# A layer of attention, convolution and feed-forward on one core: transfers in program order, and value products in three 64-column parts

## Chip, cores and metric

The kernel runs on one core of a Trainium2 chip. The metric is the device time of one execution in microseconds (us). A core has TensorE (PE in the profile), VectorE (DVE), ScalarE (ACT), GpSimd (POOL) and SyncE (SP), which here does nothing but issue DMA transfers. Weight loads of TensorE have a row of their own, PEld.

## What is computed

One layer over 2048 tokens of width 1024: an RMSNorm, one projection to three groups of heads, a norm per head on what they give, an output projection, a residual sum, then a second RMSNorm and a SwiGLU feed-forward part of width 2816. Four heads do stick-breaking attention over all earlier keys, eight heads do softmax attention over a band of 576 keys with a bias that depends on distance, and 256 channels pass a short gated convolution.

```
h = rmsnorm(x, attn_norm_w); q_a, k_a, v_a, q_b, k_b, v_b, g_b, g_c, x_c = split(h @ w_in)
y = concat(stick_breaking(q_a, k_a, v_a), chunked_relpos(norm(q_b), norm(k_b), v_b, rel_bias), short_conv(g_b, g_c, x_c))
x = x + group_rmsnorm(y) @ w_out
x = x + (silu(r @ w_gate) * (r @ w_up)) @ w_down,   r = rmsnorm(x, ffn_norm_w)
```

## The kernel before

Numbers of 32 bits are carried as pairs of 16-bit numbers, a high and a low part, and a product is made of three: high by high, high by low, low by high. The tokens lie in reverse order, in four groups of 512 or sixteen tiles of 128, and the attention part works in two halves of two groups each.

Two things are woven together (`weave`, L941). One is the stream of projections (`fill`, L900): for each half the values, queries and keys, the convolution, then the output projection of the first half (`out_proj`, L858). The other is a line of attention pieces (`attend`, L788): a stick-breaking tile of 128 queries is cut into pieces of up to four key blocks (`stick_tile`, L713), a softmax tile is one piece of up to five (`chunk_tile`, L754). Half 0 has 112 pieces and half 1 has 176, so there are 288. A stage (`stage`, L978) has three beats; with each beat every open piece that is due is carried on by one step, and then a third of the stage's share of projection work is written down. A planned clock counts the cost of that work, and `later` (L895) puts something off until the planned clock is so much further. In this part PE's instructions run in the order in which they are written down; the line that says so is

```
with tc.manual_schedule(engines={mybir.EngineType.PE}):
    weave()
```

The streams of all other engines, SP among them, are ordered by the framework's scheduler, which may take a later load ahead of an earlier store that is not ready. When the weaving is over, `stream.paced` is false and the feed-forward part (`ffn`, L1020) and the output projection of the second half are written down plainly and ordered by the scheduler.

A softmax piece runs so: scores in PSUM (L704, L707), bias and maximum on VectorE (L766), exponential on ScalarE (L773), the reciprocal of the row sum times a scale into `f` (L777, L778), then `turned` (L650): PE transposes the weights into one of two `tp` banks (L660), ScalarE copies the high part (L664), VectorE makes the low part (L669) and with it frees the bank. `weighted` (L673) multiplies by the values: for each block of 128 keys the high weights by both parts of the values side by side, 128 columns (L679), and the low weights by the values' high part, 64 columns (L684). The `av` bank, of which there is one, then has two halves. `put_y` (L689) copies it to `yu` with the factor `f` on ScalarE (L694), which frees the bank, adds the halves on GpSimd (L696) and issues the store to `ydr` (L697). `yu` has two buffers, `f` has four.

Transfers that the steps below speak of: at a head's start `attend` issues K (L798, L800), V (L801, L803), the bias of a softmax head (L806), and for each group four transfers of q (L818); scores that use them are written down two beats later. `Rows` (L420) fetches blocks of x (L478), of the normed y (L486) or of the residual (L881), and they are squared (L368), scaled (L373) and transposed (L329). `Weights` (L204) loads a block of a weight two blocks ahead (L223), squares it (L249), splits it (L274 to L276), stores the parts (L277) and reads them back in the second half (L236). Stores: q, k parts (L533), v parts (L553), the convolution (L643), normed y (L844) and the residual (L872), for which x is loaded at L868. Squares of q and k are made on GpSimd (L579) and summed on VectorE (L583).

Of the kernel before, what the change touches and what calls it, by code (L numbers as in the profile page):

```python
# [20 lines left out]
HD = 64  # L21
# [19 lines left out]
def trunk(ctx: ExitStack, tc: tile.TileContext, x, anw, w_in, qnw, knw, biasx, conv_w, onw, w_out,  # L41
# [162 lines left out]
    class Weights:  # L204
# [22 lines left out]
        def split(self, n):  # L227

            if n >= len(self.plan) or n in self.ready:
                return  # L230
            key = self.plan[n]
            if key in wd and n not in self.raw:
                made = []
                for t in wd[key]:
                    w = wp.tile([128, 2, D], F16, name="w16", tag="w16")
                    nc.sync.dma_start(w, t)  # L236
                    made.append(w)
                self.ready[n] = made
                return
            self.load(n)  # L240
            shape, one, gain, srcs = block(key)
            tiles = self.raw.pop(n)
            self.ready[n] = made = []
            m = len(tiles)
            c = 1 if one else m
            ss = small(2, "ws", BF16)
            for i, raw in enumerate(tiles):
                with nc.allow_low_precision(reason="a bound, to a factor of two"):
                    nc.scalar.activation(junk(), raw, AF.Square, accum_out=ss[:, i:i + 1])  # L249
            yield 3.0  # L250
            o, bk = tpb()
            if one:
                for i in range(m):
                    nc.tensor.matmul(o[:, 0:1], ones, ss[:, i:i + 1], start=i == 0, stop=i == m - 1)
            else:
                nc.tensor.matmul(o[:, 0:m], ones, ss[:, 0:m], start=True, stop=True)
            t = small(2, "wt")
            sc = small(2, "wsc")
            nc.vector.tensor_scalar(t[:, :c].bitcast(I32), o[:, :c].bitcast(I32), 24, None,
                                    op0=ALU.logical_shift_right)  # L260
            nc.vector.tensor_scalar(sc[:, :c].bitcast(I32), t[:, :c].bitcast(I32), -1.0, 204.0,
                                    op0=ALU.mult, op1=ALU.add)
            nc.vector.tensor_scalar(sc[:, :c].bitcast(I32), sc[:, :c].bitcast(I32), 23, None,  # L263
                                    op0=ALU.logical_shift_left)
            ds = consts.tile([128, 2], F32, name=f"ds{len(DS)}")
            nc.vector.reciprocal(ds[:, :c], sc[:, :c])
            nc.vector.tensor_scalar(ds[:, :c], ds[:, :c], INV[gain], None, op0=ALU.mult)
            bk.done = True
            DS[key] = ds, one
            wd[key] = [dp.tile([128, 2, D], F16, name=f"wd{len(wd)}_{i}") for i in range(m)]  # L270
            for i, raw in enumerate(tiles):
                yield 1.5
                w = wp.tile([128, 2, D], F16, name="w16", tag="w16")
                nc.scalar.activation(raw, raw, AF.Copy, scale=sc[:, 0:1] if one else sc[:, i:i + 1])  # L274
                nc.scalar.copy(w[:, 0, :], raw)  # L275
                nc.gpsimd.tensor_tensor(w[:, 1, :], raw, w[:, 0, :], ALU.subtract)  # L276
                nc.sync.dma_start(wd[key][i], w)  # L277
                made.append(w)

        def start(self, n, after=0.0):  # L280
# [202 lines left out]
    def y_rows(H, groups):  # L483
# [4 lines left out]

        return Rows(H, groups, fetch)

    def behind(what):
        if stream.paced:
            later(0.8, what)
        else:
            what()
# [10 lines left out]
                           lambda k: hl[:, k, :], KT)  # L506
            behind(bk.read(lambda g=g, o=o: use(g, o)))

    def proj_N(H, groups, units, use, prep=None):

        for g in groups:
            hh, hl = H.get(g, (None, None))
            for t in range(0, 4, 2):
                if prep is not None:
                    yield from prep.need(g, t)
                    hh, hl = H[g]
                o, bk = acc()
                steps = chain.from_iterable(
                    mm3(o[:, s * 256:(s + 1) * 256], lambda k, cs=cs: hh[:, k, cs],
                        lambda k, cs=cs: hl[:, k, cs], lambda k: units[k // 4][0][:, k % 4],  # L520
# [5 lines left out]
    def put_parts(src, pair, g, d, scale):  # L526

        half, c = where(g)
        st = ap.tile([128, 2, 520], F16, name="st", tag="w2")[:, :, :GRP]
        nc.scalar.activation(st[:, 0, :], src, AF.Copy, scale=scale)  # L530
        nc.vector.scalar_tensor_tensor(st[:, 1, :], src, scale, st[:, 0, :], op0=ALU.mult, op1=ALU.subtract)
        for part in range(2):
            nc.sync.dma_start(d[pair, half, part][:, c:c + GRP], st[:, part, :])  # L533

    def v_block(H, groups, W, c0, head0, prep=None):

# [7 lines left out]
        def use(g, t, o):  # L544
# [5 lines left out]
                                           op0=ALU.mult, op1=ALU.subtract)  # L550
            hf, c = where(g)
            b = c // 128 + t
            nc.sync.dma_start(vd[head0, hf][:, b:b + 2], st)  # L553

        yield from proj_N(H, groups, units, use, prep)

# [49 lines left out]
    def conv_block(H, groups, W, b, between=None):  # L606
# [28 lines left out]
        def finish(g, t1):  # L635
# [4 lines left out]
            nc.scalar.copy(yc[:, :512], tp)  # L640
            bk.done = True
            for i in range(4):
                nc.sync.dma_start(ydr[g * 4 + i][:, 768 + 128 * b:896 + 128 * b], yc[:, i * 128:(i + 1) * 128])  # L643

        u = W.get(("cx", b))
        yield from proj_T(H, groups, u[0], use_gc)
# [25 lines left out]

    def weighted(av, wh, wl, vs, first, last):  # L673


        n = len(vs)

        def high(i):
            nc.tensor.matmul(av, wh[:, i * 128:(i + 1) * 128], vs[i], start=first and i == 0,  # L679
                             stop=last and i == n - 1 > 0)  # L680

        high(0)
        for i, v in enumerate(vs):
            nc.tensor.matmul(av[:, :HD], wl[:, i * 128:(i + 1) * 128], v[:, 0, :], start=False,  # L684
                             stop=last and n == 1)
        for i in range(1, n):
            high(i)

    def put_y(T, head, av, f):  # L689
        av, bk = av  # L690
        yield
        bk.done = True
        u = ap.tile([128, 2 * HD], F32, name="yu", tag="yu")
        nc.scalar.activation(u, av, AF.Copy, scale=f)  # L694
        yield
        nc.gpsimd.tensor_tensor(u[:, :HD], u[:, :HD], u[:, HD:], ALU.add)  # L696
        nc.sync.dma_start(ydr[T][:, head * HD:(head + 1) * HD], u[:, :HD])  # L697

    def scores(Q, cols, K, k0, n, diagonal=False):

# [7 lines left out]
        return z[:, :n], bk  # L708

    def open_av():  # L710
        return bank("av", 1, 2 * HD)

    def stick_tile(T, head, K, k0, Q, V, cols):  # L713

# [39 lines left out]
    def chunk_tile(T, head, K, k0, Q, V, cols, bias):  # L754
# [3 lines left out]
        def steps():  # L758
# [14 lines left out]
            nc.scalar.activation(s[:, :n * 128], s[:, :n * 128], AF.Exp, bias=nm, scale=qks[:, 1:2],  # L773
                                 accum_out=tot)
            yield 2
            f = small(1, "f")
            nc.vector.reciprocal(f, tot)  # L777
            nc.vector.tensor_tensor(f, f, VS[head], ALU.mult)  # L778
            yield 3
# [52 lines left out]
    def y_norm(T, yt, gain, tmp):  # L832
# [8 lines left out]
        yv = yt.rearrange("p (n d) -> p n d", d=HD)  # L841
        nc.vector.tensor_tensor(yv, yv, r[:, :, None].to_broadcast([128, 16, HD]), ALU.mult)
        nc.gpsimd.tensor_tensor(yt, yt, gain, ALU.mult)
        nc.sync.dma_start(ynd[T], yt)  # L844

    def y_norms(half):
        assert traced[half] == 0, (half, traced)
# [10 lines left out]
    def out_proj(H, groups, W, prep, rows):  # L858

        for g in groups:  # L860
            for cb in range(4):
                cc = slice(cb * 256, (cb + 1) * 256)
                units = W.get(("o", cb))

                def use(g, t, o, cb=cb, cc=cc):
                    xs = xp.tile([128, 2, 256], F32, name="xs", tag="xs", bufs=2)
                    T = g * 4 + t
                    nc.sync.dma_start(xs, x[T * 128:T * 128 + 256, cc].rearrange("(b p) c -> p b c", p=128))  # L868
                    nc.vector.scalar_tensor_tensor(xs, o.rearrange("p (b c) -> p b c", b=2),
                                                   descale(("o", cb), 0), xs, op0=ALU.mult, op1=ALU.add)  # L870
                    for b in range(2):
                        nc.sync.dma_start(x1d[T + b][:, cc], xs[:, b, :])  # L872

                yield from proj_N(H, [g], units, use, prep if cb == 0 else None)
                if g == groups[-1] and cb in (1, 2) and len(groups) > 1:
                    yield from rows.ahead()

# [128 lines left out]
    with tc.tile_pool(name="ap", bufs=1) as ap0:  # L1006

        class _Pool:
            BUFS = dict(k=2, q=4, be=5, re=2, w2=8, wth=3, wtl=3, v=2, vst=1, yu=2, bias=2)

            def tile(self, shape, dt, name, tag):
                return ap0.tile(shape, dt, name=name, tag=tag, bufs=self.BUFS[tag])

        ap = _Pool()
        with tc.manual_schedule(engines={mybir.EngineType.PE}):
            weave()

    fp = ctx.enter_context(tc.tile_pool(name="fp", bufs=1))
# [121 lines left out]
```

## Time and profile before

| what | us |
|---|---|
| median of three runs | 2697.05 (2690.57 to 2703.49) |
| the profiled execution, its own time | 2698.59 |
| its span, first to last instruction | 2696.8 |
| PE busy in the span | 2526.3 |
| VectorE, ScalarE, GpSimd busy | 1458.7, 1074.8, 398.8 |
| mean granted TensorE clock, share of full | 0.982 |

An engine's busy time in a stretch is read beside the stretch's length. The table of waits names an engine's instruction, what ended its wait, the total, the times and the longest wait. The timeline has one line for each instruction or for several of the same line in a row: start, time, engine, line, operation, what is written from what; a wait of the engine just before stands in brackets. A matmul's time is that of one product from its start to its end, and products overlap, so the distance between starts tells the pace.

### The profile page before, as it was taken

What the parts mean: (1) busy time and instruction counts of PE and PEld (TensorE: products, weight loads), DVE (VectorE), ACT (ScalarE), POOL (GpSimd) and SP (SyncE); (2) the same over time, 40 slices, a digit from 0 to 9 for tenths busy, and PEclk for the clock granted to TensorE, in tenths of its full rate; (3) what the DMA queues carried; (4) which work ended last, traced back from release to release, by engine and by line L of the source; (5) the groups of instructions that cost most, each with busy time, mean ns of one, the idle gap of its engine ahead of it and who ended that gap; (6) DMA issues with size and microseconds to landing.
All of it is one profiled execution on the core that took longest, in us unless ns stands there. A gap on an engine that the chain in (4) does not pass through costs nothing.

```text
span 2696.8 us, 41816 instructions
## 1 busy us (share of the span) xinstructions
PE 2526.3 (94%) x16258; PEld 1687.1 (63%) x16258; DVE 1458.7 (54%) x3343; ACT 1074.8 (40%) x1994; POOL 398.8 (15%) x469
## 2 busy tenths in 40 slices
PE   6998889998799888979999999999999999999999
PEld 4477766666686677745555555557865555555556
DVE  6478777689988977834444334334332333223233
ACT  5575756666456776752333333321121111111110
POOL 2234331102312122121111111110000000000000
PEclk9999999999999999989999999999999999999999
DMA  7443444533321356472222233222651111111101
GB/s 260 133 131 100 132 134 143 142 110 124 105 81 43 97 152 198 120 268 105 94 94 94 94 103 113 90 102 107 223 194 39 47 47 51 66 47 48 47 24 63
DMA packets 245350, 294.31 MB, mean 109 GB/s; under 512 B 77472, under 2 KB 194208, under 8 KB 245152
## 3 DMA queue, kind: packets, MB, share of 16 engines
q1 hardware_dynamic: 245152, 291.65, 33.5%
q8 instruction: 127, 2.08, 0.3%
q14 instruction: 71, 0.58, 0.1%
HBM read 199.30 MB, written 92.27 MB: 108 GB/s over the span
## 4 chain that ended last, share of the span: by engine, by line
PE 38%; DMA 4%; issue 4%; DVE 2%; POOL 1%; ACT 1%; SPq 1%; POOLq 0%; DVEq 0%; ACTq 0%
PE acc L381 7%; PE acc L380 7%; PE acc L379 7%; PE sc L1057 5%; PE sc L1058 5%; PE sc L1059 5%; DMA x1d<-xs 1%; POOL w L276 1%; DMA wr<-in_w_down 1%; DMA wr<-in_w_up 1%; DMA xf<-x1d 0%; PE sc L329 0%; DVE gl L1042 0%; DVE x L1061 0%; DVE wl L314 0%
## 5 line engine op out<-in xcount | busy, mean ns | idle before, releaser
L381 PE MATMUL acc<-hh,w 128*128 128x512 f16 x1728 | 656.3, 380 | 0.8 <-POOL w L276 0.8
L379 PE MATMUL acc<-hh,w 128*128 128x512 f16 x1728 | 656.5, 380 | 0.4 <-ACT hh L332 0.4
L380 PE MATMUL acc<-hl,w 128*128 128x512 f16 x1728 | 656.4, 380 | 0.1
L1038 DVE SCALAR_TENSOR_TENSOR sg<-acc,ds,sg 128x512 f32<-128x512 f32 x88 | 66.0, 750 | 622.9 <-PE acc L381 548.8
L379 PE MATMUL acc<-w,hh 128*128 128x256 f16 x1408 | 391.6, 278 | 5.8 <-ACT w L275 4.2
L380 PE MATMUL acc<-w,hh 128*128 128x256 f16 x1408 | 391.5, 278 | 1.8 <-POOL w L276 1.8
L381 PE MATMUL acc<-w,hl 128*128 128x256 f16 x1408 | 391.0, 278 | 1.5 <-DVE hl L333 0.8
L1061 DVE TENSOR_TENSOR x<-sc,x 128x512 f32<-128x512 f32 x352 | 241.2, 690 | 200.9 <-PE sc L1059 194.1
L381 PEld LDWEIGHTS <-w 128*128 128x128 f16 x1728 | 169.1, 98 | 206.4 <-issue 2.0
L379 PEld LDWEIGHTS <-w 128*128 128x128 f16 x1728 | 169.3, 98 | 184.9 <-issue 7.2
L380 PEld LDWEIGHTS <-w 128*128 128x128 f16 x1728 | 169.2, 98 | 180.3 <-issue 1.1
L1057 PE MATMUL sc<-wh,gh 128*128 128x512 f32 x704 | 278.7, 396 | 3.0 <-DVE x L1061 3.0
L1058 PE MATMUL sc<-wl,gh 128*128 128x512 f32 x704 | 274.4, 390 | 0.0
L1059 PE MATMUL sc<-wh,gl 128*128 128x512 f32 x704 | 274.3, 390 | 0.0
L276 POOL TENSOR_TENSOR w<-wr,w 128x1024 f16<-128x1024 f32 x76 | 163.4, 2164 | 550.6 <-ACT w L275 515.0
L669 DVE SCALAR_TENSOR_TENSOR wtl<-tp,wth 128x512 f16<-128x512 f32 (+3 forms) x384 | 198.4, 532 | 41.8 <-ACT wth L664 40.4
L733 DVE TENSOR_TENSOR_SCAN re<-re,zero 128x512 f32<-128x512 f32 (+3 forms) x160 | 192.6, 1203 | 39.7 <-ACT re L730 39.2
L664 ACT ACTIVATE wth<-tp 128x512 f16<-128x512 f32 (+3 forms) x384 | 173.6, 476 | 87.3 <-PE tp L660 86.0
L1041 ACT CAST gh<-sg 128x512 fp32r<-128x512 f32 x88 | 54.3, 617 | 385.3 <-DVE sg L1038 385.3
L274 ACT ACTIVATE wr<-wr,wsc 128x1024 f32<-128x1024 f32 x76 | 84.4, 1146 | 202.0 <-DVE wsc L263 201.8
L380 PEld LDWEIGHTS <-hh 128*128 128x128 f16 x1408 | 140.5, 100 | 31.7 <-issue 5.5
L679 PE MATMUL av<-v,wth 128*128 128x128 f16 x1104 | 144.0, 224 | 16.3 <-ACT yu L694 16.2
(168 smaller groups left out, 3724.3 us busy)
## 6 DMA issues: line engine op xcount, KB each, us to landing
w<-wd SPq DMA_DIRECT2D x92, 512.0 KB, 4.0
wd<-w SPq DMA_DIRECT2D x76, 512.0 KB, 2.9
wr<-in_w_down SPq DMA_DIRECT2D x44, 512.0 KB, 4.4
q<-qd SPq DMA_DIRECT2D x192, 64.0 KB, 2.3
wr<-in_w_gate SPq DMA_DIRECT2D x22, 512.0 KB, 4.5
wr<-in_w_up SPq DMA_DIRECT2D x22, 512.0 KB, 5.3
xt<-in_x SPq DMA_DIRECT2D x16, 512.0 KB, 5.2
wr<-in_w_in SPq DMA_DIRECT2D x16, 512.0 KB, 5.1
```

The costliest lines, as they stand in the source:

```text
L276: nc.gpsimd.tensor_tensor(w[:, 1, :], raw, w[:, 0, :], ALU.subtract)
L379: nc.tensor.matmul(o, sh(k), mh(k), start=(k == 0), stop=False)
L380: nc.tensor.matmul(o, sh(k), ml(k), start=False, stop=False)
L381: nc.tensor.matmul(o, sl(k), mh(k), start=False, stop=(k == n - 1))
L664: nc.scalar.activation(wh[:, b0 * 128:b1 * 128], tp[:, :(b1 - b0) * 128], AF.Copy, scale=WSC)
L669: nc.vector.scalar_tensor_tensor(wl[:, s], tp[:, :(b1 - b0) * 128], WSC, wh[:, s], op0=ALU.mult, op1=ALU.subtract)
L679: nc.tensor.matmul(av, wh[:, i * 128:(i + 1) * 128], vs[i], start=first and i == 0, stop=last and i == n - 1 > 0)
L733: nc.vector.tensor_tensor_scan(re, re, zero.to_broadcast([128, N]), 1.0 if b == T else e[:, 0:1], ALU.mult, ALU.add)
L1057: nc.tensor.matmul(o, gh[:, cs], wh[:, cc], start=st, stop=False)
L1058: nc.tensor.matmul(o, gh[:, cs], wl[:, cc], start=False, stop=False)
L1059: nc.tensor.matmul(o, gl[:, cs], wh[:, cc], start=False, stop=en)
L1061: nc.vector.tensor_tensor(x1, o, x1, ALU.add)
```

## The change

SP is put under the written order too, so transfers are issued as they are written down. To keep a store from standing in front of loads, `store` puts it off by 1.5 to 5 us of the planned clock while the weaving is paced. Loads of x for the residual are written down ahead of their products, with three buffers. The products with the values become three of 64 columns for each block, `av` and `yu` have 64 columns, the sum of halves is gone, and the store of `yu` is written down two beats behind the copy. `yu` has four buffers and `f` eight.

```diff
-                nc.sync.dma_start(wd[key][i], w)
+                store(5.0, wd[key][i], w)
...
+    def store(after, dst, src):
+
+        if stream.paced:
+            later(after, lambda: nc.sync.dma_start(dst, src))
+        else:
+            nc.sync.dma_start(dst, src)
...
                 o, bk = acc()
+                if pre is not None:
+                    pre(g, t)
...
-            nc.sync.dma_start(d[pair, half, part][:, c:c + GRP], st[:, part, :])
+            store(2.0, d[pair, half, part][:, c:c + GRP], st[:, part, :])
...
-            nc.sync.dma_start(vd[head0, hf][:, b:b + 2], st)
+            store(2.0, vd[head0, hf][:, b:b + 2], st)
...
-                nc.sync.dma_start(ydr[g * 4 + i][:, 768 + 128 * b:896 + 128 * b], yc[:, i * 128:(i + 1) * 128])
+                store(1.5, ydr[g * 4 + i][:, 768 + 128 * b:896 + 128 * b], yc[:, i * 128:(i + 1) * 128])
...
-        def high(i):
-            nc.tensor.matmul(av, wh[:, i * 128:(i + 1) * 128], vs[i], start=first and i == 0,
-                             stop=last and i == n - 1 > 0)
-
-        high(0)
         for i, v in enumerate(vs):
-            nc.tensor.matmul(av[:, :HD], wl[:, i * 128:(i + 1) * 128], v[:, 0, :], start=False,
-                             stop=last and n == 1)
-        for i in range(1, n):
-            high(i)
+            c = slice(i * 128, (i + 1) * 128)
+            nc.tensor.matmul(av, wh[:, c], v[:, 0, :], start=first and i == 0, stop=False)
+            nc.tensor.matmul(av, wl[:, c], v[:, 0, :], start=False, stop=False)
+            nc.tensor.matmul(av, wh[:, c], v[:, 1, :], start=False, stop=last and i == n - 1)
...
-        u = ap.tile([128, 2 * HD], F32, name="yu", tag="yu")
+        u = ap.tile([128, HD], F32, name="yu", tag="yu")
         nc.scalar.activation(u, av, AF.Copy, scale=f)
-        yield
-        nc.gpsimd.tensor_tensor(u[:, :HD], u[:, :HD], u[:, HD:], ALU.add)
-        nc.sync.dma_start(ydr[T][:, head * HD:(head + 1) * HD], u[:, :HD])
+        yield 2
+        nc.sync.dma_start(ydr[T][:, head * HD:(head + 1) * HD], u)
...
-        return bank("av", 1, 2 * HD)
+        return bank("av", 1, HD)
...
-            f = small(1, "f")
+            f = sp.tile([128, 1], F32, name="f", tag="f", bufs=8)
...
-        nc.sync.dma_start(ynd[T], yt)
+        store(4.0, ynd[T], yt)
...
-                def use(g, t, o, cb=cb, cc=cc):
-                    xs = xp.tile([128, 2, 256], F32, name="xs", tag="xs", bufs=2)
+                XS = {}
+
+                def pre(g, t, cc=cc, XS=XS):
                     T = g * 4 + t
-                    nc.sync.dma_start(xs, x[T * 128:T * 128 + 256, cc].rearrange("(b p) c -> p b c", p=128))
+                    XS[t] = xp.tile([128, 2, 256], F32, name="xs", tag="xs", bufs=3)
+                    nc.sync.dma_start(XS[t], x[T * 128:T * 128 + 256, cc].rearrange("(b p) c -> p b c", p=128))
...
-                        nc.sync.dma_start(x1d[T + b][:, cc], xs[:, b, :])
+                        store(1.5, x1d[T + b][:, cc], xs[:, b, :])
...
-            BUFS = dict(k=2, q=4, be=5, re=2, w2=8, wth=3, wtl=3, v=2, vst=1, yu=2, bias=2)
+            BUFS = dict(k=2, q=4, be=5, re=2, w2=8, wth=3, wtl=3, v=2, vst=1, yu=4, bias=2)
...
-        with tc.manual_schedule(engines={mybir.EngineType.PE}):
+        with tc.manual_schedule(engines={mybir.EngineType.PE, mybir.EngineType.SP}):
```

## Rows read from the trace of the kernel before

**Rows 1.** Windows: busy us (instructions) of each engine, granted clock, DMA share, GB/s.
```profile
0.00:1170.00 1170.00, 1033.56 (x9032) 788.67 (x9033) 917.12 (x2397) 752.51 (x1538) 294.61 (x421) 0.97 0.43 131
1170.00:2700.00 1530.00, 1492.77 (x7228) 898.40 (x7226) 541.60 (x947) 322.31 (x456) 104.18 (x48) 0.99 0.27 92
```

**Rows 2.** Waits of PE, 0 to 1170 us: total us, times, longest.
```profile
PE tp L660 <- DVE wtl L669: 54.4, 37, 4.6
...
PE av L679 <- ACT yu L694: 16.2, 10, 3.5
```

**Rows 3.** Waits of ACT, DVE and POOL, 0 to 1170 us.
```profile
ACT junk L249 <- DMA wr<-in_w_in: 43.8, 17, 6.3
...
DVE f L777 <- ACT yu L694: 28.3, 31, 4.4
...
DVE qa L583 <- POOL qs L579: 19.3, 16, 3.3
...
POOL yu L696 <- ACT yu L694: 317.1, 116, 12.2
```

**Rows 4.** Waits of SP's queue, 0 to 1170 us.
```profile
SPq L697 <- POOL yu L696: 320.4, 133, 15.0
```

**Rows 5.** Timeline around 1044 us: start, us, instruction, wait in brackets.
```profile
1044.38 0.37 ACT L694 ACTIVATE yu<-av,f 128x128 f32<-128x128 f32 x1 [4.85 <-DMA ydr<-yu]
...
1044.78 0.16 DVE L777 RECIPROCAL f<-tot 128x1 f32<-128x1 f32 x1 [3.30 <-ACT yu L694]
...
1044.79 0.22 PE L679 MATMUL av<-v,wth 128*128 128x128 f16 x1 [2.50 <-ACT yu L694]
```

**Rows 6.** Timeline of PE around 642 and 650 us.
```profile
641.43 0.27 PE L379 MATMUL acc<-w,hh 128*128 128x256 f16 x1
...
642.14 0.28 PE L684 MATMUL av<-v,wtl 128*128 128x64 f16 x4
...
642.26 0.33 PE L679 MATMUL av<-v,wth 128*128 128x128 f16 x3
...
649.81 0.69 PE L660 MATMUL tp<-ident,be 128*128 128x128 f32 x2 [2.37 <-DVE wtl L669]
...
650.50 0.42 PE L380 MATMUL acc<-w,hh 128*128 128x256 f16 x1
```

**Rows 7.** Groups of instructions: line, engine, busy us, mean ns, idle before.
```profile
L679 PE MATMUL av<-v,wth 128*128 128x128 f16 x1104 | 144.0, 224 | 16.3 <-ACT yu L694 16.2
...
L684 PE MATMUL av<-v,wtl 128*128 128x64 f16 x1104 | 81.0, 196 | 0.0
...
L696 POOL TENSOR_TENSOR yu<-yu 128x64 f32<-128x64 f32 x192 | 73.9, 386 | 337.5 <-ACT yu L694 317.1 <-DMA ydr<-yu 12.0 <-PE acc L381 3.1
```

**Rows 8.** Timeline, 1023 to 1040 us: SP's issues, PE and ACT.
```profile
1024.13 0.59 SPq L798 DMA_DIRECT2D k<-kd  x1
...
1035.91 0.39 PE L679 MATMUL av<-v,wth 128*128 128x128 f16 x4
...
1036.92 0.36 ACT L694 ACTIVATE yu<-av,f 128x128 f32<-128x128 f32 x1
...
1038.41 0.39 PE L679 MATMUL av<-v,wth 128*128 128x128 f16 x4
...
1039.90 0.31 PE L704 MATMUL sc<-k,q 128*128 128x320 f16 x1 [0.78 <-DMA q<-qd]
```

**Rows 9.** DMA issues: transfer, count, KB each, median us to landing.
```profile
q<-qd SPq DMA_DIRECT2D x192, 64.0 KB, 2.3
...
xt<-in_x SPq DMA_DIRECT2D x16, 512.0 KB, 5.2
```

**Rows 10.** Timeline around 320 and 424 us.
```profile
318.36 1.05 ACT L368 ACTIVATE junk<-xt 128x1024 bf16<-128x1024 f32 x1
...
327.42 1.27 DVE L373 SCALAR_TENSOR_TENSOR xt<-xt,rry,gain 128x1024 f32<-128x1024 f32 x1
...
423.64 1.04 PE L329 MATMUL sc<-ident,xt 128*128 128x128 f32 x8
```

More of the change, by code (lines that the diff above doesn't have):

```diff
@@ L507, in proj_T, with proj_N @@
             behind(bk.read(lambda g=g, o=o: use(g, o)))
-    def proj_N(H, groups, units, use, prep=None):
+    def proj_N(H, groups, units, use, prep=None, pre=None):
         for g in groups:
@@ L863, in out_proj, with use @@
                 units = W.get(("o", cb))
-                def use(g, t, o, cb=cb, cc=cc):
-                    xs = xp.tile([128, 2, 256], F32, name="xs", tag="xs", bufs=2)
+                XS = {}
+                def pre(g, t, cc=cc, XS=XS):
                     T = g * 4 + t
-                    nc.sync.dma_start(xs, x[T * 128:T * 128 + 256, cc].rearrange("(b p) c -> p b c", p=128))
+                    XS[t] = xp.tile([128, 2, 256], F32, name="xs", tag="xs", bufs=3)
+                    nc.sync.dma_start(XS[t], x[T * 128:T * 128 + 256, cc].rearrange("(b p) c -> p b c", p=128))
+                def use(g, t, o, cb=cb, cc=cc, XS=XS):
+                    xs = XS[t]
+                    T = g * 4 + t
                     nc.vector.scalar_tensor_tensor(xs, o.rearrange("p (b c) -> p b c", b=2),
@@ L871, in use @@
                     for b in range(2):
-                        nc.sync.dma_start(x1d[T + b][:, cc], xs[:, b, :])
-                yield from proj_N(H, [g], units, use, prep if cb == 0 else None)
+                        store(1.5, x1d[T + b][:, cc], xs[:, b, :])
+                yield from proj_N(H, [g], units, use, prep if cb == 0 else None, pre)
                 if g == groups[-1] and cb in (1, 2) and len(groups) > 1:
```

## The prediction, made before the changed kernel ran

> **What bounds the kernel now.** I first cut the span at 1170 us, where the woven part (projections, attention, first output projection) gives way to the feed-forward part. The windows [rows 1] show TensorE (PE) busy 1492.8 of 1530 us behind the cut: that part is bound by PE, and the change hardly reaches it, because stores are delayed only while the weaving is paced. Ahead of the cut PE is busy 1033.6 of 1170 us, so 136 us are idle, at a mean granted clock of 0.97: about another 35 us. No other engine is full there (VectorE 917, ScalarE 753, GpSimd 295). The woven part is a chain of waits in an order that is written out by hand for PE, and everything at stake lies in those 171 us.
>
> Then the table of waits for the same stretch. PE waits mostly for the VectorE instruction that frees a transpose bank (54.4 us at L660) and 16.2 us for the ScalarE copy that frees the one `av` bank [rows 2]. One step further back [rows 3]: VectorE waits 28.3 us for that copy before it may write a new `f` (four buffers); VectorE waits 19.3 us for GpSimd's squares, and GpSimd, which works in order, has stood 317.1 us in front of the sums of halves; weight squares on ScalarE wait 43.8 us for loads. On SP's queue the stores stand in front of the loads: 320.4 us waiting for those sums [rows 4]. One place shows how it hangs together [rows 5]: a copy waits 4.85 us for the store of an older `yu` (two buffers), `f` 3.30 us for the copy, PE 2.50 us for the bank.
>
> The clock is a cost of its own: after a wait of 2.37 us a 256-column product takes 0.42 us, at other places 0.27 [rows 6]. The engine had fallen from 2.4 to 1.2 GHz. Over the part, 35 us lost on 136 idle is 0.26 us for each idle us.
>
> **The change part by part.**
> Products. A block of 128 keys now costs a 128-column product and a 64-column one. Three products of the first kind take 0.33 us with a tail of 0.22, so (330 - 220) / 2 = 55 ns apart; four of the second take 0.28 with 0.196, so (280 - 196) / 3 = 28 ns apart, each with its own weight load [rows 6, 7]. Before: 55 + 28 = 83 ns; after, three of 64 columns: 84. Times 1104 blocks: +1 us, and I put +2 for the loads. The other end is a product with a new weight load that goes no faster than a 128-column one: 3 x 55 = 165 ns, +82 x 1104 = +91 us. I take the near end, since the 28 ns row is the same instruction with weights of the same size.
> The Trainium skill, "TensorE: Matmul & The Clock Gate", section "Back-to-back issue gap", speaks against the change: it gives about 81 ns for a load and product pair of 128 columns in a stream of such pairs. By that, as an estimate, three pairs for two would add 81 x 1104 = 89 us; the trace's 55 and 28 ns speak against the rule here.
>
> Sum of halves and copy. 73.9 us of GpSimd work go, 192 x 386 ns [rows 7], and the ScalarE copy of 0.37 us [rows 5] halves its columns. Nothing of either is on the path by itself; it lies beside PE. I count the copy at 0 (ends: 0 and 192 x 0.37 = 71 us). What it gives is order: squares no longer queue behind a sum that waits for the copy. Of VectorE's 19.3 us [rows 3] I take 11 (ends 0 and 19).
> Four `yu` of half the width, and the store without the sum before it: of PE's 16.2 us [rows 2] I take 15 (ends 0 and 16).
> Eight `f`: of VectorE's 28.3 us [rows 3] I take 13, since PE is behind VectorE in only part of the stages (ends 0 and 28).
> Loads no longer stuck behind stores: of ScalarE's 43.8 us for weights [rows 3] I take 7; most lies in the start, or under work (ends 0 and 44).
> Clock: the net fall in idle time, 46 gained less 30 lost (next), times 0.26 is 4.
>
> SP in program order takes something away. Now SP issues loads as soon as a buffer is free: one head's K began to go out at 1024.13, its first scores ran at 1039.90 [rows 8], nearly 16 us later. Afterwards K, V, bias and q stand two beats, two thirds of a stage, in front of their scores. A stage is 1170 / 288 = 4.1 us at most, 2.5 us where tiles follow freely (1035.91 to 1038.41 [rows 8]): the place gives 2.7 or 1.7 us. An issue takes about 0.6 us (K 0.59 [rows 8]), and q lands 2.3 us later [rows 9]. In front of the scores stand 7 transfers (half 0, stick), 8 (half 0, chunk), 10 and 11 (half 1), and 4 at a head's second group. What counts is how far SP runs ahead of PE. A `yu` store stands a stage behind its product, and its data are made 1.0 us after the product (1036.30 to 1037.28 [rows 8]): 1.5 to 3 us of slack, and 1 to 2 us of program since the last store's place. I take 4 us. Then a head waits 11 x 0.6 + 2.3 - 1.7 - 4 = 3.2 us, eight times; with 10, 1.8 four times (2.5 us of place); with 8, 0.4 eight times; the others nothing: 36 us. Ends: 0, and 188 if SP is level with PE.
> Row blocks. A first pair of rows of x or of the residual is now fetched at its use, at four places. The second half's x now had its squares at 318.36 and its transposes at 423.64 [rows 10]. Landing 5.2 us [rows 9], squares of 1.05 each [rows 10], and the scaling after them, say 4: 11 us, less 4, less 0 to 2.6 of place: 6 each, 24 us. Ends: 0, and 4 x 15.5 = 62, where 15.5 is 5.2 plus the 10.3 from the first square to the first scaled row in a crowded stretch (318.36 to 328.69). In return, that work leaves the crowd on VectorE around 325 us; I count nothing for it.
> Of 36 + 24 = 60 I take half, 30: a PE that waits for q lets VectorE catch up, and part of a wait [rows 2] is paid once.
> The order of VectorE, ScalarE and GpSimd is not written by hand and is made anew; no row prices that. I take 0, ends a gain or a loss of half of the 54.4 us. The residual's x goes out ahead of its products, its stores 1.5 us behind theirs: nothing, hidden by 48 products.
>
> Sum: 15 + 13 + 11 + 7 + 4 = 50 gained; 30 + 2 = 32 lost; 18 us faster. The profiled execution took 2698.59 us (1.8 outside its span), 1.5 above the median of 2697.05: 2698.6 - 18 = 2680.6, so **2680**.
>
> **Rivals.**
> *Nothing to be measured.* SP is 3 us ahead. The heads cost 8 x 4.2 + 4 x 2.8 + 8 x 1.4 + 4 x 0.8 = 59, the rows 28; half is 44, plus 2. That eats the 46 gained, and the clock gives nothing: **2699**. For it: stores of q, k and v parts are put off by 2.0 us only, which must cover their making. Against: the `yu` stores, the most frequent, have more.
> *Loads too late, slower.* The mechanism is the same wait, at a head's first scores. At 2 us ahead heads and second groups cost 42 + 15 + 19 + 7 + 8 = 91, rows 32; half is 61, plus 2 and 4 for the clock, less 46: 21 slower, **2720**. It decides from about 3 us down. For it: today PE lost only 0.78 us to q at 1039.90 [rows 8], and that only because SP runs far ahead. Against: a store that is made in time holds nobody.
> *Products bound by weight loads.* +91 in place of the 2 that I put: 2680.6 + 89, about **2770**. Against it stands the row of 28 ns.
> *More is gained.* VectorE's and ScalarE's waits go whole and the clock stays up: about 2650, with the forecast's mechanism.
>
> **How the numbers follow.** Forecast with its larger variant 0.44; nothing to be measured 0.28; late loads 0.25; weight loads 0.03. A measurement of this kernel can tell about 0.5% (13.5 us) from no change, so faster 0.44, same 0.28, slower 0.28. The forecast's own range is 2650 to 2683. Both signs hold weight, so the whole range goes from 2640 to 2735: it takes in the late loads at 2720 and 15 us beyond, and leaves out some 0.08 below and 0.12 above.
>
> **What would show it.** Right: no `f` wait for `yu`; no wait of the copy for a store; the sums gone; PE's wait for `av` near zero; products of 64 columns 28 ns apart; PE waits for q and K of some 10 to 35 us in all; idle time ahead of the feed-forward part down by about 15 us. Wrong: waits for q and K over 60 us, or PE standing for transposes of x for 10 us a place (late loads); 64-column products 50 ns apart; PE's wait for transpose banks as large as now, which would mean that VectorE's work itself, not its waits, held PE.

## The result, and the profile after

The changed kernel is slower, where 2680 us were forecast:

| what | before | after |
|---|---|---|
| median, us (4 runs each on one chip) | 2700.27 (2690.57 to 2703.49) | 2789.45 (2788.34 to 2792.22) |
| ratio | 1 | 1.0338, interval 1.0308 to 1.0368 |
| span of the profiled execution, us | 2696.8 | 2790.4 |
| mean granted TensorE clock | 0.982 | 0.969 |
| first product of the feed-forward part, us | 1156.7 | 1242.8 |

All but 7.5 us of the loss lie ahead of the feed-forward part: 1242.8 - 1156.7 = 86.1 us of 2790.4 - 2696.8 = 93.6. In the table of waits of PE, 0 to 1260 us of the kernel after, one line that stood near nothing before is now the largest (the ones of before are [rows 2]):

```profile
PE sc L705 <- DMA q<-qd: 43.6, 17, 5.8
PE tp L669 <- DVE wtl L678: 35.2, 35, 3.1
PE sc L329 <- DVE xt L373: 34.4, 4, 14.8
PE sc L705 <- DMA ydr<-yu: 21.1, 7, 5.7
PE sc L329 <- DVE xf L373: 11.5, 1, 11.5
...
PE sc L708 <- DMA q<-qd: 4.6, 11, 1.0
PE av L687 <- ACT yu L696: 4.5, 6, 2.0
```

L705 and L708 are the score products (L704 and L707 before). A score reads only K and q, so I take the line that names a `ydr` store for the same wait, put down to another transfer (the experiment with the heads' loads ahead confirms it): together 43.6 + 21.1 + 4.6 = 69.3 us of waiting for loads of heads and groups. Below them stand transposes of `xt` and of `xf`, blocks of x and of the residual. What was to fall fell: the wait for `av` from 16.2 to 4.5 us and that for transpose banks from 54.4 to 35.2 [rows 2]. That is 31 us won in these lines, against 69 + 46 in the others, of which 17 us for `xt` and 1 us for q stood there before; 22.5 of the 34.4 us for `xt` lie in the first 70 us, where all 17.2 of before lay.

The timeline of the kernel after shows how one head comes late (start, us, instruction, wait in brackets; products and copy of an earlier tile, SP's issues, then PE, POOL and DVE; the head is of the kind of that in [rows 8], two heads earlier):

```profile
1022.37 0.19 PE L687 MATMUL av<-v,wth 128*128 128x64 f16 x1
...
1022.40 0.19 PE L688 MATMUL av<-v,wtl 128*128 128x64 f16 x1
...
1022.43 0.19 PE L689 MATMUL av<-v,wth 128*128 128x64 f16 x1
...
1024.22 0.29 ACT L696 ACTIVATE yu<-av,f 128x64 f32<-128x64 f32 x1
...
1024.54 0.32 SPq L698 DMA_DIRECT2D ydr<-yu  x1
1024.91 0.45 SPq L799 DMA_DIRECT2D k<-kd  x1
1025.42 0.59 SPq L801 DMA_DIRECT2D k<-kd  x1
...
1027.98 1.59 SPq L804 DMA_DIRECT2D v<-vd  x1
1029.66 0.45 SPq L807 DMA_DIRECT2D bias<-in_rel_bias  x1
1030.16 2.37 SPq L819 DMA_DIRECT2D q<-qd  x4
...
1034.08 0.42 PE L705 MATMUL sc<-k,q 128*128 128x320 f16 x1 [5.76 <-DMA q<-qd]
...
1039.88 0.30 PE L705 MATMUL sc<-k,q 128*128 128x320 f16 x1
...
1033.41 1.88 POOL L808 TENSOR_SCALAR bias<-bias,qks 128x640 f32<-128x640 f32 x1 [10.35 <-DMA bias<-in_rel_bias]
...
1035.54 0.15 POOL L810 MEMSET bias<- 64x64 f32 x1
...
1035.90 0.49 DVE L767 CUSTOM_DVE_ANT_0 s<-sc,bias 128x320 f32<-128x320 f32 x1 [5.52 <-PE sc L708]
```

SP issued a store at 1024.54, right after the copy that made its data ended (1024.22 + 0.29 = 1024.51), and the head's K right behind that store. SP was no further than ScalarE's copy. The head's eleven transfers then took SP until 1030.16 + 2.37 = 1032.53, and the first scores ran at 1034.08, after a PE wait of 5.76 us. In [rows 8] K went out at 1024.13 and was needed at 1039.90, 15.8 us later; here 9.2 us lie between, and they are all SP's own time and the landing. PE had nothing else to do from 1034.08 - 5.76 = 1028.32 on, 3.4 us after K went out. It is not that all of a head's transfers went out early before: the last two of q of that head, too, left SP only about 1 us ahead of the scores.

```profile
1036.14 2.77 SPq L818 DMA_DIRECT2D q<-qd  x2
```

What had gone out early there were K, V, the bias and two of q, nine of the eleven transfers. On the row of the head's first scores stands the price of the wait in clock: the score of 320 columns took 0.42 us, the same product without a wait at 1039.88 0.30.

VectorE, GpSimd and SP in their tables of waits, 0 to 1260 us of the kernel after:

```profile
DVE s L767 <- POOL bias L810: 48.0, 13, 6.6
DVE f L778 <- ACT s L774: 46.1, 85, 2.2
...
DVE qa L592 <- POOL qs L588: 17.5, 18, 2.0
...
POOL bias L808 <- DMA bias<-in_rel_bias: 259.9, 12, 42.3
...
SPq L698 <- ACT yu L696: 391.7, 126, 14.1
```

`f` no longer waits for the copy of `yu`, but for the exponential whose row sum it needs: 46.1 us in place of 28.3 [rows 3]. The squares' wait (17.5 for 19.3) stayed. A wait that stood in no row of before is VectorE's for the bias, 48.0 us: the bias comes in with the head, GpSimd scales it in 1.88 us and clears two corners, and only then may VectorE add it to the scores. At the head above it was ready at 1035.54 + 0.15 = 1035.69, just as late as the scores, and VectorE had stood for 5.52 us. And SP stands 391.7 us in front of `yu` stores, where it stood 320.4 [rows 4]; what has changed is that the loads behind them can no longer go first.

The windows, cut at each kernel's first feed-forward product (columns as in [rows 1]); after:

```profile
0.00:1242.80 1242.80, 1047.97 (x10077) 799.82 (x10078) 925.47 (x2389) 736.57 (x1529) 211.49 (x226) 0.94 0.39 121
1242.80:2790.40 1547.60, 1518.18 (x7287) 905.10 (x7285) 547.80 (x954) 330.28 (x466) 111.84 (x52) 0.99 0.27 93
```

and before, cut in the same way:

```profile
0.00:1156.70 1156.70, 1021.03 (x8974) 783.12 (x8975) 912.52 (x2389) 744.63 (x1529) 286.98 (x418) 0.97 0.43 130
1156.70:2696.80 1540.10, 1505.30 (x7287) 903.96 (x7284) 546.20 (x954) 330.19 (x466) 111.81 (x52) 0.99 0.27 94
```

PE's idle time in the woven part went from 1156.7 - 1021.0 = 135.7 to 1242.8 - 1048.0 = 194.8 us, and the clock from 0.97 to 0.94. In the feed-forward part PE is busy 1518.2 in place of 1505.3 us with the same 7287 products: 13 us that the prediction did not have, and that are in the products themselves, since waits are not counted as busy. The part grew by 7.5 us only, because its idle time fell from 34.8 to 29.4 us.

### The profile page after: what moved, and what is told of

Same layout as the page of the kernel before. It is cut to its first block, busy times and chain, and to the rows that moved or that the text cites. A ratio compares the mean times of both kernels' runs of the same rounds, so it can differ in the third digit from the quotient of the medians.

```text
span 2790.4 us, 43760 instructions
## 1 busy us (share of the span) xinstructions
PE 2566.1 (92%) x17362; PEld 1704.9 (61%) x17362; DVE 1473.3 (53%) x3343; ACT 1066.9 (38%) x1994; POOL 323.3 (12%) x277
## 5 line engine op out<-in xcount | busy, mean ns | idle before, releaser
L379 PE MATMUL acc<-w,hh 128*128 128x256 f16 x1408 | 395.8, 281 | 4.5 <-ACT w L275 4.1
L380 PE MATMUL acc<-w,hh 128*128 128x256 f16 x1408 | 395.5, 281 | 1.8 <-POOL w L276 1.8
L705 PE MATMUL sc<-k,q 128*128 128x320 f16 (+4 forms) x384 | 124.7, 330 | 69.8 <-DMA q<-qd 43.6
```

The costliest lines, as they stand in the source:

```text
L379: nc.tensor.matmul(o, sh(k), mh(k), start=(k == 0), stop=False)
L380: nc.tensor.matmul(o, sh(k), ml(k), start=False, stop=False)
L705: nc.tensor.matmul(z[:, :n], q1[:, cols], kc, start=True, stop=False)
```

## The experiments

Ratios are against the kernel before, run on the same chip beside each group of kernels. The woven part's end is the start of the first feed-forward product.

### SP free again

```diff
-        with tc.manual_schedule(engines={mybir.EngineType.PE, mybir.EngineType.SP}):
+        with tc.manual_schedule(engines={mybir.EngineType.PE}):
```

> The changed kernel, with SP's stream given back to the framework's scheduler; products, buffers and put-off stores stay. Theory A (loads that go out only at their place make PE wait at a head's first scores and at the row blocks, and the clock falls behind those waits): the 90 us go and the relief of f, yu and the sums shows, 2660 to 2700 us; PE's waits for q under 5 us. Theory B (three products with a weight load each): 2760 to 2790. Theory C (the put-off stores themselves): still above 2740.

Measured: 2687.69 us (2682.89 to 2691.03), ratio 0.9988 (0.9975 to 1.0002). One word takes back 1.0338 - 0.9988 = 3.5 points, some 94 us. The table of waits of PE to 1145 us has no line for q:

```profile
PE tp L669 <- DVE wtl L678: 45.8, 38, 4.7
PE sc L329 <- DVE xt L373: 17.4, 3, 14.8
PE av L687 <- ACT yu L696: 10.7, 8, 3.3
```

So the loss hangs on SP's order and not on the products. It does not yet say which transfers.

### The products alone

```diff
-            nc.tensor.matmul(av[:, :HD], wl[:, i * 128:(i + 1) * 128], v[:, 0, :], start=False,
-                             stop=last and n == 1)
...
+            c = slice(i * 128, (i + 1) * 128)
+            nc.tensor.matmul(av, wh[:, c], v[:, 0, :], start=first and i == 0, stop=False)
+            nc.tensor.matmul(av, wl[:, c], v[:, 0, :], start=False, stop=False)
+            nc.tensor.matmul(av, wh[:, c], v[:, 1, :], start=False, stop=last and i == n - 1)
...
-        u = ap.tile([128, 2 * HD], F32, name="yu", tag="yu")
+        u = ap.tile([128, HD], F32, name="yu", tag="yu")
...
-        nc.gpsimd.tensor_tensor(u[:, :HD], u[:, :HD], u[:, HD:], ALU.add)
```

This is the kernel before with three products of 64 columns, `av` and `yu` of 64 columns and no sum of halves; two `yu` and four `f`, SP free.

> The kernel before with the three 64-column products alone: av and yu of 64 columns, no sum of halves, the store right behind the copy; two yu, four f, SP ordered by the scheduler. Theory A: 2680 to 2705 us, 64-column products 28 ns apart. Theory B: 2770 to 2790.

Measured: 2677.68 us (2673.89 to 2679.27), ratio 0.995 (0.9931 to 0.9969); the woven part ends at 1141.2 us, 15.5 earlier. Its waits to 1142 us, PE and then DVE:

```profile
PE tp L660 <- DVE wtl L669: 51.6, 36, 4.6
...
PE av L678 <- ACT yu L687: 11.4, 9, 2.4
...
DVE f L769 <- ACT yu L687: 21.8, 38, 1.9
```

The split products, the narrower copy and the missing sum are together worth half a per cent. This run does not say how much each of them gives; that the split itself costs next to nothing is read from the distance of 28 to 30 ns between the products' starts.

### The transfers alone

The reverse: the changed kernel with the old products, the sum, two `yu` and four `f`. The store of `yu` stands behind the sum again, one beat after the copy and not two.

```diff
-            nc.tensor.matmul(av, wh[:, c], v[:, 1, :], start=False, stop=last and i == n - 1)
+            nc.tensor.matmul(av[:, :HD], wl[:, i * 128:(i + 1) * 128], v[:, 0, :], start=False,
+                             stop=last and n == 1)
...
+        nc.gpsimd.tensor_tensor(u[:, :HD], u[:, :HD], u[:, HD:], ALU.add)
...
-            f = sp.tile([128, 1], F32, name="f", tag="f", bufs=8)
+            f = small(1, "f")
```

> The changed kernel with the old products, the sum of halves, two yu and four f: only the transfers' order, the put-off stores and the early x of the residual differ from before. Theory A: slower than the changed kernel, 2790 to 2840 us, since the sums now hold SP's queue too. Theory B: back to 2690 to 2710.

Measured: 2794.32 us (2792.78 to 2801.99), ratio 1.0391 (1.0369 to 1.0414). The transfers' order makes 3.9% of loss without the new products; the products, with their buffers and the later store, take 1.0391 - 1.0338 = 0.5 points off it, as much as the products took off with SP free. So far as these runs tell, the two halves of the change add up.

### V behind q

A head's V is first used after its transposes, later than q. Here only its place moves, from ahead of bias and q to behind the first group's q.

```diff
-        nc.sync.dma_start(V[:, :HT // 128], vd[head // 4 * 4, half][:, :, head % 4])
-        if more:
-            nc.sync.dma_start(V[:, HT // 128:], vd[head // 4 * 4, 0][:, :more // 128, head % 4])
...
+            if g == groups[0]:
+                nc.sync.dma_start(V[:, :HT // 128], vd[head // 4 * 4, half][:, :, head % 4])
+                if more:
+                    nc.sync.dma_start(V[:, HT // 128:], vd[head // 4 * 4, 0][:, :more // 128, head % 4])
```

> The changed kernel with V's loads behind the q of a head's first group: one or two transfers fewer in front of the first scores, nothing else moved. Theory A: each costs its issue of 0.6 us: 1.2 us at each of 12 heads of half 1, 0.6 at 12 of half 0, some 18 us off the gaps of 68 us at first scores and 5 to 10 off the clock's share, 2755 to 2775 us. Theory C (the stores hold SP): 2785 to 2795.

Measured: 2753.02 us (2746.83 to 2753.6), ratio 1.022 (1.0203 to 1.0236): 1.0338 - 1.022 = 1.2 points, 32 us, at the upper end of what was expected. In the waits of PE to 1210 us the heads' line is down:

```profile
PE sc L705 <- DMA q<-qd: 34.9, 21, 3.8
```

From 43.6 + 21.1 to 34.9 is 30 us of waiting, for one transfer fewer in front of the scores of 12 heads and two fewer at the other 12: 30 / 36 = 0.8 us for each. In the timeline above the two issues of V took 0.55 and 1.59 us. So PE waits for SP's own time in front of the scores.

### Heads' loads one group of tiles ahead

SP stays in the written order, but K, V, bias and q of the next head, or q of the next group, are written down at the third of the four tiles of the group before (the loop over `t` runs from 3 down to 0).

```diff
+                if t == 1:
+                    if g != groups[-1]:
+                        ahead[half, head, groups[-1]] = load_q(half, head, groups[-1])
+                    elif head < 11 and (half, (head + 1) // 2 if head + 1 < 4 else 2 + (head - 3) // 2) in done:
+                        ahead[half, head + 1] = load_head(half, groups, head + 1)
+                        ahead[half, head + 1, groups[0]] = load_q(half, head + 1, groups[0])
```

> The changed kernel, SP in program order, but K, V, bias and q of the next head, or q of its second group, are written down at the third of four tiles of the group before. Theory A: PE's waits for q and K (68 us of gaps at first scores) and VectorE's 48 us for the bias go nearly whole; 2700 to 2730 us, what is left being the row blocks (some 30 us with the clock). Theory C (SP is held up by its stores, wherever the loads stand): 2760 or more.

Measured: 2720.03 us (2717.41 to 2721.38), ratio 1.0108 (1.009 to 1.0126): 2.3 points back, 62 us. Waits of PE to 1175 us:

```profile
PE tp L669 <- DVE wtl L678: 38.5, 38, 3.3
PE sc L329 <- DVE xt L373: 37.4, 4, 14.7
PE sc L329 <- DVE xf L373: 17.9, 1, 17.9
```

Of the lines for q 3.5 us are left, and none names the `ydr` store any more, so that one was indeed K and q. The wait of VectorE for the bias fell from 48.0 to 3.5 us with it. The waits for rows of x and of the residual stayed.

### The first row blocks ahead too

The same kernel, in which the rows of x (both halves) and of the normed y always have their next pair of blocks on the way, also from one group to the next; and the first pair of the second half's x, of y and of the residual, with the gain row where there is one, is fetched before it is due.

```diff
+        def first(self):
+            self.get(*self.todo[0])
+            if self.norm is not None:
+                self.norm.gain()
...
+                elif self.early and self.todo:
+                    self.get(*self.todo[0])
...
+                if g == groups[-1] and cb == 1 and len(groups) > 1 and stream.paced:
+                    rows.first()
...
+                if p == 3:
+                    rows[half + 1].first()
```

> The run with the heads' loads written ahead (2720 us there), and now the first row blocks of x, of the normed y and of the residual, and their gain rows, are written down a stage or more ahead of their use as well. Theory A: what was left of the loss was the row blocks (PE's waits for xt 37.4 and xf 17.9 us there, 15 of it the start): 2680 to 2695 us, PE's wait for xf under 5 us ahead of the feed-forward part. Rival: SP in written order costs something beyond late loads: 2705 us or more.

Measured: 2687.26 us (2680.95 to 2691.23, 10 runs), ratio 0.998 (0.9966 to 0.9993): another 1.3 points, 34 us. The woven part ends at 1136.7 us, earlier than in any kernel with SP free. Waits for `xt` are down to 23.7 us, and 21.9 of them lie in the first 60 us of the kernel. There the kernel before had 17.2, so some 5 us more are left; the third and fourth pair of x go out from 28.26 us on, and from 10.91 on in the kernel before.

### Eight `f` in the kernel before

The kernel with heads and rows ahead is still 10 us slower than the products alone, though its woven part ends 4.5 us earlier; the loss lies behind. The feed-forward part has no code of the change in it, but eight `f` in place of four move every buffer that is laid out after them by 4 x 32 = 128 bytes (an `f` takes 32 bytes of each partition).

```diff
-            f = small(1, "f")
+            f = sp.tile([128, 1], F32, name="f", tag="f", bufs=8)
```

> The kernel before with eight buffers of f and nothing else. In the runs so far the feed-forward's third kind of product (f32, 512 columns) takes 401/395 ns with eight f and 396/390 with four, whatever else differs; eight f move every later buffer up by 128 bytes. Theory P (the place of the buffers): 401/395 ns here too, the feed-forward part 11 us longer, and the woven part a few us shorter: 2690 to 2702. Rival (f has no part in it): 396/390, and 2680 to 2690 by the relief of VectorE.

Measured: 2699.11 us (2692.93 to 2704.21, 10 runs), ratio 1.0026 (1.0013 to 1.0039). Its woven part ends 2.8 us earlier than before, and yet it is slower. Of the groups of instructions, this is the first of the three products of the feed-forward part's 32-bit values, in the kernel before and in this one:

```profile
L1057 PE MATMUL sc<-wh,gh 128*128 128x512 f32 x704 | 278.7, 396 | 3.0 <-DVE x L1061 3.0
```

```profile
L1057 PE MATMUL sc<-wh,gh 128*128 128x512 f32 x704 | 282.0, 401 | 2.7 <-DVE x L1061 2.7
```

396 ns became 401, and the two products beside it 395 for 390. From start to start it is 226 to 227 ns before and 230 to 232 after: some 5.5 ns x 2112 products = 11.6 us, and nothing waits.

### Products, four `yu` and 68 `f`

If the place is the cause, 60 further buffers of `f` (2048 bytes in all in place of 128) may bring the pace back while `f` has more than enough buffers. This is the kernel of the products alone with four `yu` and 68 `f`.

```diff
-            f = small(1, "f")
+            f = sp.tile([128, 1], F32, name="f", tag="f", bufs=68)
...
-            BUFS = dict(k=2, q=4, be=5, re=2, w2=8, wth=3, wtl=3, v=2, vst=1, yu=2, bias=2)
+            BUFS = dict(k=2, q=4, be=5, re=2, w2=8, wth=3, wtl=3, v=2, vst=1, yu=4, bias=2)
```

> The kernel with the three products alone (2677.7 us), with four yu and 68 f: the f then move later buffers up by 2048 bytes, a whole number of the product's own rows of 512 f32. Theory P: 396/390 ns, and the relief of yu and f comes on top: 2660 to 2675 us. Rival: the product's pace depends on something else than the 128 bytes: 401/395 and 2680 to 2690.

Measured: 2677.15 us (2671.45 to 2679.76), ratio 0.994 (0.9924 to 0.9955), with 396 and 390 ns. Against 2677.68 with two `yu` and four `f` that is nothing; the 2660 to 2675 that were expected with the buffers' relief on top were missed. The buffers that were to relieve `f` and the copy are worth nothing on PE's path. The waits of VectorE to 1143 us say why:

```profile
DVE f L769 <- ACT s L765: 37.2, 69, 3.7
```

Where `f` waited 21.8 us for the copy of `yu`, it now waits for the row sum, which the scores set.

### The placed version, in order

The kernel with heads and rows ahead, and 68 `f`.

```diff
-            f = sp.tile([128, 1], F32, name="f", tag="f", bufs=8)
+            f = sp.tile([128, 1], F32, name="f", tag="f", bufs=68)
```

> The kernel of e5_rows (SP in the written order, the heads' loads and the first row blocks written ahead) with 68 buffers of f in place of 8: 60 more buffers of 32 bytes, so that every later buffer stands 1920 bytes further, 2048 and not 128 bytes off the places that it would have with f's four. Nothing else changes. Placement theory: the products of the feed-forward part take 396 and 390 ns again in place of 401 and 395, that part is some 11 us shorter, the woven part ends where it did (1137 us, within 4): 2687 - 11 = 2676, within 4, about 0.5 to 0.6% under the kernel before. Rival, that the pace hangs on SP's order or on the stores issued in it, not on the place: 401 and 395 ns stay, and the time stays at 2687, within 4.

Measured: 2676.39 us (2669.39 to 2683.0), ratio 0.994 (0.9923 to 0.9956), as expected for the place. Windows of the profiled execution, cut at its first feed-forward product:

```profile
0.00:1136.10 1136.10, 1010.01 (x10079) 777.61 (x10080) 918.26 (x2389) 737.27 (x1529) 212.52 (x226) 0.98 0.42 132
1136.10:2667.60 1531.50, 1504.82 (x7287) 902.94 (x7284) 547.23 (x954) 330.45 (x465) 111.78 (x52) 0.99 0.27 94
```

The feed-forward part is back at 1504.8 us busy. The transfers' order, written with their time in hand, costs nothing against a free SP, and it gives nothing that can be told from it either: 2676.39 here and 2677.15 with SP free.

### The changed kernel, placed

```diff
-            f = sp.tile([128, 1], F32, name="f", tag="f", bufs=8)
+            f = sp.tile([128, 1], F32, name="f", tag="f", bufs=68)
```

> The changed kernel with 68 buffers of f in place of 8 and nothing else: how much of its loss is placement and how much is SP's order. Placement theory with late loads: the feed-forward part's products take 396 and 390 ns, the woven part still ends at about 1243 us (within 5), the time is 2789 - 11 = 2778, within 5. Rival, that the pace hangs on SP's order: 401 and 395 ns, 2789 within 4.

Measured: 2764.36 us (2761.37 to 2774.62), ratio 1.0272 (1.0251 to 1.0293), with 396 and 390 ns. This is 14 us better than expected. The feed-forward part takes 1532.8 in place of 1547.6 us, as much as with heads and rows ahead (1531.5 in place of 1546.0); the woven part ended at 1230.1 us and not at 1243, with PE's, GpSimd's and SP's instructions in the same order. Part of that is the chip: the kernel before took 2692.07 us in this group of runs and 2700.27 beside the changed kernel. By ratio the gain is 0.66 points, 18 us, for 0.4 expected. Whether the place touches something in the woven part too was not settled; with heads and rows ahead the woven part did not move with the place (1136.7 and 1136.1).

## Why the prediction was wrong, point by point

**The account of the loss.** In points of the ratio: heads' loads 1.0338 - 1.0108 = 2.3, first row blocks 1.0108 - 0.998 = 1.3, the place of the buffers 0.998 - 0.994 = 0.4, together 4.0, or 107 us of 2690; the products give back 0.5 to 0.6, which leaves the measured 3.4. These shares hold in this order of steps: the place alone was worth 0.3 points in the kernel before and 0.7 in the changed kernel. The mechanism was named, as the rival of loads that come too late at 2720, with a chance of 0.25; its place was right (first scores of a head, transposes of x), and so were its signs (over 60 us of waits for q and K, some 10 us a place for x), its size was not. The rival nearest to 2789 in number, products bound by weight loads at 2770, had no part in it.

**The step that failed: "I take 4 us" for how far SP runs ahead, and "Of 36 + 24 = 60 I take half, 30".** The 4 us were made of a `yu` store's slack behind its product, counted from the planned places. The trace shows the store going out 0.03 us after its data (1024.51 to 1024.54): the store's place in the program was reached before its data were there, so SP stood at it, and as there are 192 of these stores, SP seldom got further than ScalarE's copies (126 waits, 391.7 us). The prediction had the sign of it in hand in [rows 4]: 320.4 us of standing in front of the very stores that were now to hold everything behind them. Delaying a store by two beats did not make up for it, as the copy itself runs that late; whether a longer delay would have done it was not run. For the eight softmax heads of the second half the prediction's own formula gave 3.2 us each, 26 in all; their waits at the first scores were 4.95, 3.01, 5.76, 3.82, 5.71, 4.72, 4.21 and 5.16 us, 37 in all. Over these eight heads issue and landing took 9.1 us on the mean, where 6.6 + 2.3 = 8.9 were priced; but K went out only 4.4 us before PE was ready for the scores, where 1.7 + 4 = 5.7 were priced. So the 4 us were 2.7. The prediction's own formula gives 59 us in all for 3 us and 91 for 2, so about 69 for 2.7, if the lead was the same at the other groups, and 69 were measured: the formula held, the lead in it did not. The other groups were priced at 10 or at nothing and made up the other 32 of 69.

**The halving.** It rested on VectorE catching up while PE waits for q, so that part of the wait for transpose banks would be paid once. That wait did fall, from 54.4 to 35.2 us, and came back to 38.5 when the heads' loads were moved ahead, and to 43.4 with the row blocks ahead as well (the placed version in order, 0 to 1140 us):

```profile
PE tp L681 <- DVE wtl L690: 43.4, 42, 3.3
```

Between the changed kernel and this one the waits for q, K, `xt` and `xf` fell by 89 us and PE's idle time in the woven part by (1242.8 - 1048.0) - (1136.1 - 1010.0) = 68.7: not half, but a little under a quarter was paid once. With the 38 us of slower products that came with the idle time (below, under the clock) the 89 us of waits made 106.7 us of the woven part.

**Row blocks.** "6 each, 24 us", halved to 12; measured 34 by the ratios of the two kernels. As waits the 24 were near: `xt` and `xf` went from 17.2 to 45.9 us, 28.7 more. The second half's x in the timeline of the kernel after:

```profile
425.10 1.92 SPq L478 DMA_DIRECT2D xt<-in_x  x4
428.75 1.06 ACT L368 ACTIVATE junk<-xt 128x1024 bf16<-128x1024 f32 x1 [0.48 <-DMA xt<-in_x]
...
435.60 0.17 DVE L370 TENSOR_SCALAR sa<-sa 128x2 f32<-128x2 f32 x1 [1.83 <-ACT junk L368]
...
436.08 0.75 DVE L358 TENSOR_SCALAR gain<-gain,gsa 128x1024 f32<-128x1024 f32 x1
...
436.86 2.48 DVE L373 SCALAR_TENSOR_TENSOR xt<-xt,rry,gain 128x1024 f32<-128x1024 f32 x2
...
438.20 1.57 PEld L329 LDWEIGHTS sc<-ident,xt 128*128 128x128 f32 x8 [9.61 <-DVE xt L373]
```

From the issue to the first transpose 13.1 us passed. Of these the first square came 3.65 us after the issue (5.2 were priced for the landing), the two squares took 2.4 (2.1 priced), and the scaling after them 7.0 where 4 were priced: ahead of the first row VectorE took the squares of the next pair of blocks, for which it had waited 1.83 us, and scaled the gain in 0.75. By then it had no attention work left to do.

**The clock.** It was counted as a gain of 4 us, by 0.26 us for each idle us less. Idle time rose, and the price was about twice as high. The changed kernel and the best in-order one run the same products up to two (10077 and 10079) in the woven part: 68.7 us of idle time went along with 1048.0 - 1010.0 = 38.0 us of busy time, 0.55 for each. Two pairs with an equal number of `f` lie on either side of it: 0.44 with eight (the changed kernel and the one with heads and rows ahead), 0.59 with 68. Of the eight heads above, six ran their first score product in 0.42 to 0.45 us and two in 0.30: after a wait of 3 to 6 us PE had mostly fallen to the lower of its two levels.

**Products: right.** 28 to 30 ns from start to start and 1104 of each of the three. The starts in the first timeline, 1022.37, 1022.40 and 1022.43, show a high product, a low one and a high one, each with a weight load of its own. The Trainium skill, "TensorE: Matmul & The Clock Gate", section "Back-to-back issue gap", gives some 81 ns for pairs of 128 columns and a floor of about 25 ns for products of 1 to 64 columns. These rows, of 64 columns with a weight load each, lie near the floor and far below the 81 ns that the estimate in the prediction took for them.

**The sum of halves, `yu` and `f`.** 15 + 13 + 11 = 39 us were put on three waits. Products without the sum gave 15.5 us of the woven part, the additional buffers nothing on top. The three waits are no three gains: a wait that ends earlier on VectorE hands over to the next one in the same chain (row sum, scores), and PE's largest line, the transpose banks, went from 54.4 to 51.6 only. For the "+7" for loads no longer behind stores no run shows a gain: ScalarE's wait for weights stayed at 43.5 us with SP free and fell to 28.5 in the changed kernel, and nothing tells whether PE gained by that.

**The bias.** That a late head would hold VectorE through GpSimd's scaling as well, 48.0 us, stood in no term.

**"The change hardly reaches" the feed-forward part.** It reaches it by 11 to 15 us through the place of its buffers: 2112 products x 5.5 ns, or the 14.8 and 14.5 us by which the two kernels with 68 `f` are shorter there.

## What to carry to other kernels

Before a queue is put into the written order, ask of every entry in it when its data are ready, not where it is written: an in-order queue that holds stores runs no further ahead than the latest store's data, and every load behind has to be written early enough to cover its own issue time, the issues in front of it and its landing. A row that says how long the queue stands in front of stores today gives the size of that. And when buffers are added or taken away, compare the mean time of the products that have nothing to do with them, since a kernel's second half can slow down without a single wait.

## What the runs showed of the hardware that was not expected

Products of 512 columns of 32-bit values are sensitive to where buffers lie. The six kernels with eight `f` (the changed one, SP free, V behind q, heads ahead, rows ahead, and the kernel before with eight `f`) show a mean of 401 or 402 ns for the first of these products; the six with four or 68 (128 bytes less, or 1920 more; a third `xs` adds 2048 in some of both) show 395 or 396, whatever SP's order, the products and the number of `yu`. The products of 16-bit values of the same width stayed at 379 or 380 ns. Of what these products read, `wh` and `wl` lie ahead of `f` in memory and do not move with it, `gh` and `gl` lie behind and do. Whether it is they, and why 128 bytes matter, is not shown.

An idle us in the woven part cost about twice as much through the clock as the prediction had taken from the trace before: 0.44 to 0.59 us of slower products for each, by three pairs of kernels.
